# Four of the eight up tiles of each first quarter computed as two seven-product pairs, in a two-layer streaming encoder on one Trainium2 core

## The chip, the core and the metric

The kernel runs on one core of one Trainium2 chip. The metric is the time of one execution on the device, in microseconds (us). The engines are called TensorE (PE in the profile, with PEld for its weight loads), VectorE (DVE), ScalarE (ACT), GpSimd (POOL) and SyncE (SP, which only issues transfers here).

## The reference, cut to what matters

The reference is one step of a two-layer encoder on 576 tokens (512 of a prompt, 64 of a running stream). Each layer has a mixer and then an MLP, and the change is in the MLP alone:

```python
def _rmsnorm(x, g):
    xf = xf * lax.rsqrt(jnp.mean(xf * xf, axis=-1, keepdims=True) + EPS)
    return (xf * g.astype(jnp.float32)).astype(x.dtype)

def _mlp(h, w_up, w_down):
    u = jax.nn.relu(h @ w_up)
    return (u * u) @ w_down
...
    x = x + _mlp(_rmsnorm(x, norm_mlp[i]), mlp_w_up[i], mlp_w_down[i]).astype(x.dtype)
```

The model width is 1024, the hidden width 4096, all in float32.

## The kernel before, in words

**Layout and precision.** x stands as eight blocks of 128 channels x 576 tokens; `HT` = 288 is half of the tokens, so that a half fits one matmul. Every operand of a product is held as two parts, an upper one (a rounded copy, made by ScalarE) and a lower one (what the rounding lost, made by a subtraction on VectorE). A product then takes three matmuls of 128x288: upper x upper, upper x lower, lower x upper. In the names, `wh` and `wl` are the parts of a weight tile of 128x512, `raw` is what a transfer loaded, `xs` are the eight blocks of x times the norm's gain, with both parts.

**The norm.** The MLP runs on x times the gain; the factor per token is multiplied in later. `Norm.add` squares the blocks of x on ScalarE and adds them up in `s2` on VectorE (L344). `Norm.stats` sums `s2` over the channels by ten small matmuls (`st`, L376), from which the factor r is made in small steps on VectorE (L398 to L403); `Norm.spread` spreads it over the partitions by a diagonal (L366, L369) and matmuls with ones (`rb`, L356), which ScalarE copies to `norm.rb` (rbm). TensorE's instructions run in their order, so the up tiles behind `st` wait for the last addition to `s2`.

**Quarters, tiles and pairs.** The hidden width is worked in four quarters of 1024, each with eight up tiles of 128 hidden channels and then four Down pairs of two output tiles. A plain up tile (`project`, L326) goes over all eight blocks of x: 8 x 3 x 2 halves = 48 matmuls. Two tiles can also be computed together as a pair of seven products instead of eight (`seven`, L528): the two tiles and the two halves of tokens make a 2 x 2 product, and sums of weight blocks and sums of x stand in the factors named b11, t1, t2, b21, t3, b22, t4. Each product is 4 blocks x 3 = 12 matmuls; the pair has 84 where two plain tiles have 96. In the first four sevens of each MLP (`SEEDED`) one matmul more seeds a bank. The products use the banks a, b and c of PSUM, the on-chip accumulator memory: the product t4 goes to the bank b that t3 had, after VectorE has read it (L669 in `Up.hi1`).

Quarters 2 to 4 use pairs both for the up tiles (class `Up`) and for Down (class `Down`). The first quarter of each MLP uses eight plain up tiles, then four Down pairs. The relu and squaring of a plain tile are in `finished`, which also makes the sums of the activations that Down needs.

**The sums of x.** A pair of up tiles needs, for each j from 0 to 3, sums of the blocks x[j] and x[4+j]. `x_sums` makes them: one ScalarE instruction, four on VectorE of 128x288 (L451 to L454), a ScalarE cast of the upper part and the lower part on VectorE (L456, 128x864). `x_difference` splits one more of them into `xs` (L313). Before the change j = 0 and 1 are made after the fourth and sixth plain tile, j = 2 and 3 between the Down pairs (`x_prepared`).

**Weights.** The list `jobs` (`mlp_jobs`) fixes the order of the loads; "up" and "down" are plain tiles, "even" and "odd" the two blocks of a pair. `Stream.fill` issues loads as buffers come free: SyncE's queue has the plain ones, and a pair also needs three sums of blocks, for which GpSimd's queue issues accumulating transfers (L235, L256). `made` yields the split units; a subtraction can be given to GpSimd by `sub=pool`. The line is L194 on either engine. In layer 0 the first three up tiles are split early, their lower parts on GpSimd.

Within the MLP the scheduler of the language sets the order on each engine, from the order of the code and the dependences; the engines then run their rows in that order.

Of the kernel before, what the change touches and what calls it, by code (L numbers as in the profile page):

```python
# [18 lines left out]
KT = D // P  # L19
# [33 lines left out]
SEEDED = 4  # L53
LEAD = 5
UP_ORDER = (0, 4, 1, 5, 2, 6, 3, 7)
FACTORS = ("t4", "t3", "t1", "t2", "b11", "b22", "b21")
FIRST_DOWN = (0, 2, 1, 3)

# [2 lines left out]
def pool_dsa_kernel(ctx: ExitStack, tc: tile.TileContext, a, o):  # L61
# [100 lines left out]
    def mlp_jobs(layer, plain=0):  # L162
        for c in range(4):
            for n, f in enumerate(UP_ORDER):
                kind = "odd" if c and n % 2 else "even" if c else "up"
                jobs.append((kind, a["w_up"][layer, c * 8 + f], KT * P))
            for m in range(KT) if c else [2 * q + i for q in FIRST_DOWN for i in range(2)]:
                kind = "down" if c == 3 and m >= KT - plain else "odd" if m % 2 else "even"
                jobs.append((kind, a["w_down"][layer, c, m], KT * P))
# [27 lines left out]
    class Stream:  # L197
# [13 lines left out]
        def fill(self):  # L211
            while jobs:
                kind, src, n = jobs[0]
                mlp = kind in MLP_BLOCKS
                room = self.room(mlp)
                if room is None:
                    return
                at, pool_, size = room
                if not self.blocks or len(self.blocks[-1][1]) == 2:
                    self.blocks.append((kind, [], src, []))  # L220
                raw = self.blocks[-1][1]
                i = len(raw)
                raw.append(raw_tile(pool_, size)[:, :n // 2])
                self.live[at].append(raw[-1])
                if kind == "w_v":
                    act.dma_start(raw[-1].rearrange("p (k c) -> p k c", k=2), src.rearrange("p (k c) -> p k c", k=4)[:, 2 * i:2 * i + 2, :256])
                else:
                    (nc.sync if mlp else act).dma_start(raw[-1], src[:, i * n // 2:(i + 1) * n // 2])
                if kind == "w_ki":
                    weigh = a["w_v"][i].rearrange("p (k c) -> p k c", k=4)[:, :, 256:]  # L230
                    act.dma_start(raw[-1].rearrange("p (k c) -> p k c", k=4)[:, :, 64:64 + NIDX], weigh)
                if kind == "even" and i == 0:
                    self.even, self.sum = src, sum_of(jobs[1][1])
                if kind == "odd" and i == 0:
                    pool.dma_start(raw[0], self.even[:, :512], accum_op=ALU.add)  # L235
                    self.blocks[-1][3].append(self.sum)
                if i:
                    jobs.pop(0)
# [20 lines left out]
    def made():  # L259

        stream = Stream()
        while True:
            block = stream.take()
            if block is None:
                return
            kind, raw = block[:2]
            if kind != "even":
                early = kind == "w_o" and turns["out"] < KT  # L270
                turns["out"] += kind == "w_o"
                for i in range(2):
                    u = split_unit(raw[i], kind == "w_kq" and i == 0 and turns["spare"] < SPARE_UNITS, pool if early or kind == "w_kq" and i else None,
                                   pool.tensor_copy if early and i else act.copy)
                    stream.done(raw[i])
                    yield u
                continue
            _, other, _, (s1,) = stream.take()
            (a11, a12), (s3, a22) = raw, other
            s2 = phase["sums"].tile([P, 512], F32, tag="sum", name=uid("sum"))  # L280
            dve.tensor_tensor(s2, s1, a11, ALU.add)
            for n, src in enumerate((a11, s1, s2, a12, s3, s2, a22)):
                u = split_unit(src)
                if n == 3:
                    dve.tensor_tensor(s2, s2, a12, ALU.add)
                if n in (0, 3, 4, 6):
                    stream.done(src)
                yield u
# [129 lines left out]
    def mlp(layer, gi, late=0, end=None):  # L418
# [23 lines left out]

            return (KT - LAST if end and c == 3 else KT) // 2

        def x_sums(j, raw, first, difference):

            t = x_sums_tile()
            xt.append(t)
            gain, minus = gv[:, gi, j:j + 1], negative[:, half + j:half + j + 1]
            act.activation(first, x[j][:, :HT], AF.Copy, scale=gain)  # L450
            dve.scalar_tensor_tensor(raw[:, 0], x[j][:, HT:], gain, first, ALU.mult, ALU.subtract)  # L451
            dve.scalar_tensor_tensor(difference, x[half + j][:, :HT], gv[:, gi, half + j:half + j + 1], first, ALU.mult, ALU.subtract)
            dve.scalar_tensor_tensor(raw[:, 1], x[half + j][:, :HT], minus, raw[:, 0], ALU.mult, ALU.subtract)
            dve.scalar_tensor_tensor(raw[:, 2], x[half + j][:, HT:], minus, raw[:, 1], ALU.mult, ALU.subtract)  # L454
            act.copy(t[:, :, 0], raw)
            dve.tensor_tensor(t[:, :, 1], raw, f32(t[:, :, 0]), ALU.subtract)  # L456

        def x_difference(j, difference):

# [251 lines left out]
        def finished(i, pt, us):  # L711
# [2 lines left out]
                pair = tiles()  # L714
            v, u = pair
            activated(pt, v[:, 5:7] if i % 2 else v[:, 1:5:3])
            if i == KT - 2:
                parts_of(u, v, slice(4, 5))
                first_sum(v)
                parts_of(u, v, slice(2, 3))  # L720
            elif i == KT - 1:
                middle_sums(v)
                parts_of(u, v, slice(1, 4, 2))
                upper(u, v, slice(5, 7))
                last_sum(v)
                lower(u, v, slice(5, 7))
                parts_of(u, v, slice(0, 1))
            elif i % 2:
                upper(u, v, slice(4, 7))
                first_sum(v)  # L730
                middle_sums(v)
# [5 lines left out]
                us.append(u)  # L737

        todo, us = [], []
        for i in range(KT):  # L740
            w = next_block()
            pt = (psum1("up"), psum1("up")) if i == 2 else psum("up")
            project(pt, w, xs, spread() if i == 2 else iter(()))
            todo.append((i, pt, us))
            if i == 1:
                norm.stats()
            if i < 2:
                continue
            for t in todo:
                finished(*t)  # L750
            todo.clear()
            if i in (3, 5):
                r = 2 * i - 6
                if i == 3:
                    snap = halves(tmp("snap", "s2", 1))
                x_sums(i // 2 - 1, rough[:, r:r + 3], rough[:, r + 3], snap[:, i // 2 - 1])

        def x_prepared(n):

            if n < 2:  # L760
                v = v_tile()
                x_difference(n, snap[:, n])
                x_sums(n + 2, v[:, :3], v[:, 3], v[:, 4])
                x_difference(n + 2, v[:, 4])

        for n, q in enumerate(FIRST_DOWN):
            seven(of(us), n == 0, Down(q))
            x_prepared(n)
        for c in range(1, 4):
            us = []  # L770
            for j in range(half):
# [930 lines left out]
```

## Time and profile before

| | us |
|---|---|
| median of 3 runs | 1071.96 (1071.82 to 1073.69) |
| profiled execution, its own time | 1070.67 |
| its span in the trace | 1068.8 |
| TensorE busy | 1046.4 |
| VectorE busy | 912.0 |
| ScalarE busy | 625.7 |
| GpSimd busy | 239.5 |

The profile is of one execution. A row of a timeline has the start in us from the span's start, the length in us, engine, line of the kernel, operation, output<-inputs, tile, xcount where equal ones are put together, and in brackets the idle time ahead of it with what ended it. A row's length reaches a little over the start of the next, so starts are compared where an instruction's cost is meant. A row of the groups has line, engine, operation, count, then the busy time and the mean of one in ns. Granted clock is the share of full speed at which TensorE was clocked.

### The profile page before, as it was taken

To read this page: it belongs to the slowest core of one execution; us is meant where nothing else is said; L and a number is where in the kernel's file an instruction comes from. 1 tells how busy PE (TensorE), PEld (TensorE's weight loads), DVE (VectorE), ACT (ScalarE), POOL (GpSimd) and SP (SyncE) were. 2 spreads that over 40 slices of the span, in tenths; PEclk is the share of its full clock that TensorE was granted. 3 is DMA by queue.
4 is the path that set the end of the run, shared out by engine and by line. 5 is a ranking of instruction groups with operands and counts; after the bars stand their busy time and mean duration, and the time that the engine had idled before them with its cause. 6 is when DMAs were issued, how large, how long until landed. Compare 5 with 4: busy or idle time off the path is not lost.

```text
span 1068.8 us, 21707 instructions
## 1 busy us (share of the span) xinstructions
PE 1046.4 (98%) x7978; PEld 1022.7 (96%) x7978; DVE 912.0 (85%) x1865; ACT 625.7 (59%) x1252; POOL 239.5 (22%) x254
## 2 busy tenths in 40 slices
PE   8999999999999999999999999999999999999996
PEld 8999999999999999999999888999999999999995
DVE  7879989879988998889999675689889879979974
ACT  8556457547646765454368776456457447547742
POOL 3200111111111110667546620000111111111101
PEclk9999999999999999999999999999999999999998
DMA  8233666676576665845552554343666676676522
GB/s 254 89 102 92 165 165 163 158 179 156 151 182 169 157 173 176 237 137 139 170 156 75 169 170 107 126 107 89 178 159 149 178 172 164 149 183 163 124 55 89
DMA packets 98027, 159.65 MB, mean 149 GB/s; under 512 B 15697, under 2 KB 29312, under 8 KB 97920
## 3 DMA queue, kind: packets, MB, share of 16 engines
q1 hardware_dynamic: 70720, 111.78, 33.2%
q0 software_dynamic: 15840, 28.84, 17.1%
q10 hardware_dynamic: 11360, 17.63, 5.1%
q8 instruction: 63, 1.03, 0.4%
q14 instruction: 44, 0.36, 0.1%
HBM read 142.99 MB, written 12.72 MB: 146 GB/s over the span
## 4 chain that ended last, share of the span: by engine, by line
PE 84%; DVE 7%; DMA 3%; issue 2%; POOL 2%; ACT 1%; SPq 0%; ACTq 0%; DVEq 0%; POOLq 0%
PE b L528 33%; PE c L528 16%; PE up L326 9%; PE a L528 8%; PE pj L326 4%; PE wo L326 2%; PE wa L326 2%; PE pb L1072 1%; PE pt L1402 1%; PE dn L326 1%; PE o L1434 1%; DVE mask L1319 1%; PE sc L1376 1%; DVE m L1318 1%; DMA raw<-in_w_in 1%
## 5 line engine op out<-in xcount | busy, mean ns | idle before, releaser
L193 ACT CAST wh<-raw 128x512 fp32r<-128x512 f32 x308 | 189.7, 620 | 208.5 <-PE b L528 65.9
L194 DVE TENSOR_TENSOR wl<-raw,wh 128x512 fp32r<-128x512 f32 x284 | 198.2, 700 | 33.6 <-ACT wh L193 29.5
L528 PE MATMUL b<-u,wh 128*128 128x288 f32 x992 | 203.3, 296 | 2.3 <-ACT a L565 1.9
L528 PEld LDWEIGHTS b<-u,wh 128*128 128x128 f32 x992 | 159.6, 188 | 4.3 <-ACT a L565 3.1
L193 ACT CAST wh<-sum 128x512 fp32r<-128x512 f32 x165 | 102.3, 620 | 95.7 <-PE b L528 41.6
L528 PE MATMUL b<-u,wl 128*128 128x288 f32 x496 | 145.9, 295 | 0.4 <-DVE wl L194 0.4
L194 DVE TENSOR_TENSOR wl<-sum,wh 128x512 fp32r<-128x512 f32 x165 | 112.2, 686 | 22.3 <-ACT wh L193 20.8
L256 POOL DMA_DIRECT2D sum<-in_w_down x31 | 27.1, 894 | 340.9 <-DMA sum<-in_w_down 102.5
L528 PE MATMUL c<-u,wh 128*128 128x288 f32 x496 | 102.7, 296 | 0.0
L528 PEld LDWEIGHTS b<-u,wl 128*128 128x128 f32 x496 | 93.5, 189 | 0.6 <-DVE wl L194 0.6
L326 PE MATMUL up<-xs,wh 128*128 128x288 f32 x512 | 89.6, 296 | 0.9 <-DVE x L1593 0.8
L494 DVE TENSOR_TENSOR u<-v,u 128x576 fp32r<-128x576 f32 (+3 forms) x106 | 83.0, 786 | 2.0 <-ACT u L491 1.6
L528 PEld LDWEIGHTS c<-u,wh 128*128 128x128 f32 x496 | 79.8, 188 | 1.3 <-ACT wh L193 1.1
L528 PE MATMUL b<-xt,wh 128*128 128x288 f32 x384 | 77.7, 296 | 0.0
L528 PE MATMUL b<-xs,wh 128*128 128x288 f32 x384 | 77.2, 295 | 0.0
L326 PEld LDWEIGHTS up<-xs,wh 128*128 128x128 f32 x512 | 74.6, 188 | 2.0 <-ACT wh L193 1.0
L491 ACT CAST u<-v 128x576 fp32r<-128x576 f32 (+3 forms) x106 | 73.7, 699 | 3.2 <-DVE v L515 2.3
L528 PE MATMUL c<-u,wl 128*128 128x288 f32 x248 | 73.1, 295 | 0.0
L256 POOL DMA_DIRECT2D sum<-in_w_up x24 | 20.8, 865 | 203.1 <-DVE wl L194 83.4
L326 PE MATMUL pj<-xs,wh 128*128 128x288 f32 x352 | 62.1, 295 | 0.0
L528 PEld LDWEIGHTS b<-xt,wh 128*128 128x128 f32 x384 | 61.5, 188 | 0.0
L528 PEld LDWEIGHTS b<-xs,wh 128*128 128x128 f32 x384 | 61.2, 188 | 0.0
(300 smaller groups left out, 2724.7 us busy)
## 6 DMA issues: line engine op xcount, KB each, us to landing
raw<-in_w_up SPq DMA_DIRECT2D x128, 256.0 KB, 3.1
raw<-in_w_down SPq DMA_DIRECT2D x128, 256.0 KB, 2.9
raw<-in_w_o ACTq DMA_DIRECT2D x32, 256.0 KB, 2.8
sum<-in_w_down SPq DMA_DIRECT2D x31, 256.0 KB, 2.9
sum<-in_w_down POOLq DMA_DIRECT2D x31, 256.0 KB, 4.7
raw<-in_w_down POOLq DMA_DIRECT2D x31, 256.0 KB, 5.0
raw<-in_w_in ACTq DMA_DIRECT2D x30, 256.0 KB, 3.0
sum<-in_w_up SPq DMA_DIRECT2D x24, 256.0 KB, 3.2
```

What stands on the lines that cost most here:

```text
L193: cast(h, src)
L194: (sub or how["sub"]).tensor_tensor(l, src, f32(h), ALU.subtract)
L256: pool.dma_start(s1, odd[:, 512:], accum_op=ALU.add)
L326: pe.matmul(pt[h][:, :m] if isinstance(pt, tuple) else pt[:, h, :m], wt, xs[k][:, part, c:c + m], start=(k == 0 and i == 0), stop=(k == n ...
L491: return act.copy(u[:, f, 0], v[:, f])
L494: return dve.tensor_tensor(u[:, f, 1], v[:, f], f32(u[:, f, 0]), ALU.subtract)
L528: ins = pe.matmul(bank[:, :HT], wt, ut, start=first and j == 0 and i == 0, stop=j == 3 and i == 2, skip_group_check=True)
L1072: pe.matmul(pt[:, c0:c0 + rhs.shape[1]], lhs, rhs, start=n == 0, stop=n == len(steps) - 1)
L1318: dve.max(m8[rows], order[rows])
L1319: dve.match_replace(order[rows], m8[rows], order[rows], TAKEN)
L1376: pe.matmul(pt[:, hh, :nw], q[:, 2 * s + hh], ks[g][:, part, :nw], start=part == 0, stop=part == 1)
L1402: pe.transpose(pp[:, c:c + P], pr[:, hh, kt * P:(kt + 1) * P], ident)
```

## The change

In each first quarter only the first four up tiles stay plain (`PLAIN_UP`); the tiles five to eight become two pairs, `Up(0, 2)` and `Up(0, 3)`. The sums of x are therefore needed earlier: `x_sums(j)` is called after each plain tile j, the differences follow the fourth, and `x_prepared` is gone. The lower part of the sums is made on GpSimd instead of VectorE (L466), and of the second, third and fourth plain tile the second half block's lower part is too (`POOLED`). In layer 0 GpSimd made both lower parts of the first three tiles before the change already. All sums go through one tile `rough`, whose slots j = 2 takes over from j = 0, and 3 from 1. The loads of the last four tiles are of the kinds "even" and "odd", and `fill` does not start a pair's loads until the pool for the sums of blocks is open.

```diff
+PLAIN_UP = 4
+POOLED = (1, 2, 3)
...
-                kind = "odd" if c and n % 2 else "even" if c else "up"
+                kind = "up" if not c and n < PLAIN_UP else "odd" if n % 2 else "even"
...
+                if kind == "even" and "sums" not in phase:
+                    return
...
+                if kind == "up":
+                    ups += 1
+                pooled = kind == "up" and (ups - 1) % PLAIN_UP in POOLED
                 for i in range(2):
-                    u = split_unit(raw[i], kind == "w_kq" and i == 0 and turns["spare"] < SPARE_UNITS, pool if early or kind == "w_kq" and i else None,
+                    u = split_unit(raw[i], kind == "w_kq" and i == 0 and turns["spare"] < SPARE_UNITS, pool if early or i and (pooled or kind == "w_kq") else None,
...
-        def x_sums(j, raw, first, difference):
+        def x_sums(j):
...
+            at = half * (1 + j % 2)
+            raw, first, difference = rough[:, at:at + 3], rough[:, at + 3], rough[:, j]
...
             act.copy(t[:, :, 0], raw)
-            dve.tensor_tensor(t[:, :, 1], raw, f32(t[:, :, 0]), ALU.subtract)
+            pool.tensor_tensor(t[:, :, 1], raw, f32(t[:, :, 0]), ALU.subtract)
...
-        for i in range(KT):
+        for i in range(PLAIN_UP):
...
-            if i < 2:
-                continue
-            for t in todo:
-                finished(*t)
-            todo.clear()
-            if i in (3, 5):
-                r = 2 * i - 6
-                if i == 3:
-                    snap = halves(tmp("snap", "s2", 1))
-                x_sums(i // 2 - 1, rough[:, r:r + 3], rough[:, r + 3], snap[:, i // 2 - 1])
...
-        for n, q in enumerate(FIRST_DOWN):
-            seven(of(us), n == 0, Down(q))
-            x_prepared(n)
+            if i >= 2:
+                for t in todo:
+                    finished(*t)
+                todo.clear()
+            x_sums(i)
+        snap = halves(tmp("snap", "s2", 1))
+        for j in range(half):
+            x_difference(j, rough[:, j])
+        for j in range(PLAIN_UP // 2, half):
+            up = Up(0, j)
+            seven(of_x, False, up)
+            us.append(up.u)
+
+        for q in FIRST_DOWN:
+            seven(of(us), q == FIRST_DOWN[0], Down(q))
```

The lines of the new kernel are shifted: the split of a weight is L196, the addition of squares L352, `x_sums` L461 to L466, the products L538, the read of bank b ahead of t4 L679.

The order shows what moves. First VectorE in layer 0, around the last additions to `s2` (s_113), as it was; `xt_...` is the scratch that holds a block's squares, `wl_...` a weight's lower part:

```order
L344 TENSOR_TENSOR s_113_641<-s_113_641,xt_674 128x576
L194 TENSOR_TENSOR wl_737<-raw_371,wh_736 128x512
L344 TENSOR_TENSOR s_113_641<-s_113_641,xt_674 128x576 x2
L344 TENSOR_TENSOR s_113_641<-s_113_641,xt_681 128x576
L194 TENSOR_TENSOR wl_743<-raw_377,wh_742 128x512
```

The same place with the change (`s_108` is the new name of `s2`, `rough` the tile of the sums of x):

```order
L352 TENSOR_TENSOR s_108_631<-s_108_631,xt_664 128x576
L463 SCALAR_TENSOR_TENSOR rough_676<-x_83,negative_674,rough_676 128x288
L324 SCALAR_TENSOR_TENSOR xs_653<-x_84,gv,xs_653 128x576
L464 SCALAR_TENSOR_TENSOR rough_676<-x_83,negative_674,rough_676 128x288
L196 TENSOR_TENSOR wl_752<-raw_371,wh_751 128x512
L462 SCALAR_TENSOR_TENSOR rough_676<-x_84,gv,rough_676 128x288 x2
L352 TENSOR_TENSOR s_108_631<-s_108_631,xt_664 128x576
L464 SCALAR_TENSOR_TENSOR rough_676<-x_83,negative_674,rough_676 128x288
L352 TENSOR_TENSOR s_108_631<-s_108_631,xt_664 128x576
L196 TENSOR_TENSOR wl_844<-raw_734,wh_843 128x512
L352 TENSOR_TENSOR s_108_631<-s_108_631,xt_671 128x576
```

Ten sums of x (five of them ahead of this piece) and one more lower part of a weight now stand ahead of the last addition.

GpSimd after the change, from the end of the weights that it split early, in layer 0:

```order
L260 DMA sum_950<-in_w_down 128x512
L239 DMA raw_741<-in_w_up 128x512
L196 TENSOR_TENSOR wl_758<-raw_377,wh_757 128x512
L466 TENSOR_TENSOR xt_726<-rough_676,xt_726 128x3x288
L239 DMA raw_761<-in_w_up 128x512
L466 TENSOR_TENSOR xt_833<-rough_676,xt_833 128x3x288
L466 TENSOR_TENSOR xt_931<-rough_676,xt_931 128x3x288
L466 TENSOR_TENSOR xt_1012<-rough_676,xt_1012 128x3x288
L260 DMA sum_1180<-in_w_down 128x512
```

Before, only transfers stood here; now one lower part of a weight and the four of the sums do, and the accumulating transfers queue between them.

TensorE after the change, around the last plain tile of layer 0; `rb` are the matmuls that spread r, `b_1031` is the first product of the first pair, which the scheduler put ahead of that tile, `a_1032` the seed:

```order
L334 MATMUL up_854<-xs_653,wl_396 128x288
L364 MATMUL rb_888<-xt_671,ones 128x288
L364 MATMUL rb_891<-xt_671,ones 128x288
L538 MATMUL b_1031<-xs_632,wh_843 128x288 x2
L538 MATMUL b_1031<-xs_632,wl_844 128x288
...
L538 MATMUL b_1031<-xs_641,wl_844 128x288
L574 MATMUL a_1032<-xs_632,wh_843 128x288
L334 MATMUL up_953<-xs_632,wh_751 128x288 x4
```

Before, the matmuls rb stood inside the third tile and the fourth followed it directly; now rb follows the third tile, and thirteen matmuls of the pair come between rb and the fourth.

More of the change, by code (lines that the diff above doesn't have):

```diff
@@ L263, in made @@
         stream = Stream()
+        ups = 0
         while True:
@@ L716, in finished @@
             activated(pt, v[:, 5:7] if i % 2 else v[:, 1:5:3])
[L717 to L728, printed above, removed]
+            if i % 2:
                 upper(u, v, slice(4, 7))
@@ L746, in mlp @@
                 norm.stats()
-            if i < 2:
-                continue
-            for t in todo:
-                finished(*t)
-            todo.clear()
-            if i in (3, 5):
-                r = 2 * i - 6
-                if i == 3:
-                    snap = halves(tmp("snap", "s2", 1))
-                x_sums(i // 2 - 1, rough[:, r:r + 3], rough[:, r + 3], snap[:, i // 2 - 1])
[L758 to L764, printed above, removed]
-        for n, q in enumerate(FIRST_DOWN):
-            seven(of(us), n == 0, Down(q))
-            x_prepared(n)
+            if i >= 2:
[12 more added lines that the diff above has]
+            seven(of(us), q == FIRST_DOWN[0], Down(q))
         for c in range(1, 4):
```

## The prediction

> **What bounds the kernel now.** I read the page first, for which engine sets the end, then the busy time of each engine in the two stretches that the change touches, then the timeline of TensorE and VectorE in them.
>
> ```profile
> span 1068.8 us, 21707 instructions
> ...
> PE 1046.4 (98%) x7978; PEld 1022.7 (96%) x7978; DVE 912.0 (85%) x1865; ACT 625.7 (59%) x1252; POOL 239.5 (22%) x254
> ...
> PE 84%; DVE 7%; DMA 3%; issue 2%; POOL 2%; ACT 1%; SPq 0%; ACTq 0%; DVEq 0%; POOLq 0%
> ```
>
> TensorE is busy for 98% of the span and carries 84% of the chain that ended last. A matmul taken away is worth its time, if whatever feeds TensorE keeps up. The second view has the stretch of the first quarter's up tiles in layer 0 (41.0 to 95.3) and in layer 1 (679 to 737); its columns are length, busy PE, PEld, DVE, ACT and POOL with counts, granted clock, DMA share and GB/s.
>
> ```profile
> 41.00:95.30 54.30, 54.22 (x407) 53.55 (x406) 44.64 (x78) 29.21 (x49) 2.61 (x3) 1.00 0.29 79
> ...
> 679.00:737.00 58.00, 57.22 (x425) 56.36 (x426) 42.36 (x78) 29.18 (x49) 2.59 (x3) 1.00 0.34 92
> ```
>
> TensorE has no gap there, but VectorE is busy for 82% of the first stretch. GpSimd, which takes the new work, does almost nothing. The change therefore asks whether VectorE, made to do its work earlier, stays ahead of TensorE. The timeline shows how far ahead it is in layer 0.
>
> ```profile
> 41.38 0.77 PE L326 MATMUL up<-xs,wh 128*128 128x288 f32 x4
> ...
> 54.15 1.34 PE L376 MATMUL st<-ones,s 128*128 128x96 f32 x10
> 55.41 0.80 PE L326 MATMUL up<-xs,wh 128*128 128x288 f32 x4
> ...
> 60.67 1.13 PE L356 MATMUL rb<-xt,ones 128*128 128x288 f32 x4
> 61.43 0.51 PE L326 MATMUL up<-xs,wh 128*128 128x288 f32 x1
> ...
> 47.56 0.69 DVE L194 TENSOR_TENSOR wl<-raw,wh 128x512 fp32r<-128x512 f32 x1
> 48.16 2.34 DVE L344 TENSOR_TENSOR s<-s,xt 128x576 f32<-128x576 f32 x3
> 50.42 0.68 DVE L194 TENSOR_TENSOR wl<-raw,wh 128x512 fp32r<-128x512 f32 x1
> ```
>
> The statistics matmuls (st) at 54.15 need the last addition of the squares, which is over by 50.42. The slack is 3.7 us. In layer 1 it is much larger, 691.99 less 681.46:
>
> ```profile
> 680.71 0.75 DVE L344 TENSOR_TENSOR s<-s,xt 128x576 f32<-128x576 f32 x1
> ...
> 691.99 1.34 PE L376 MATMUL st<-ones,s 128*128 128x96 f32 x10
> 693.25 0.80 PE L326 MATMUL up<-xs,wh 128*128 128x288 f32 x4
> ```
>
> **The matmuls saved.** Between 41.38 and 54.15 two plain tiles, 96 matmuls, pass: 12.77 us / 96 = 0.133 us each. Two plain tiles become one pair of seven products, 7 x 12 = 84 matmuls, so a pair saves 12 x 0.133 = 1.6 us. There are two pairs in each of the two MLPs: 3.2 us a layer, **-6.4 us** in all. The seed matmul goes with the first four sevens of an MLP wherever they are, and their number stays.
>
> **What VectorE now does ahead of the statistics, layer 0.** By the order, ten of the sums of x (L461 to L464) and one more subtraction of a weight's lower part stand ahead of the last addition of squares. Their durations, start to start:
>
> ```profile
> 73.70 0.52 DVE L451 SCALAR_TENSOR_TENSOR rough<-x,gv,rough 128x288 f32<-128x288 f32 x1
> 74.14 0.51 DVE L452 SCALAR_TENSOR_TENSOR snap<-x,gv,rough 128x288 f32<-128x288 f32 x1
> ...
> 80.88 1.05 DVE L456 TENSOR_TENSOR xt<-rough,xt 128x864 fp32r<-128x864 f32 x1
> 81.85 0.45 DVE L502 TENSOR_TENSOR v<-v 128x288 f32<-128x288 f32 x1
> ```
>
> A sum takes 0.43 us, and the subtraction 48.16 - 47.56 = 0.60. Ten and one make 4.9 us, so the last addition is over at 55.3 in place of 50.42, and TensorE, which is there at 54.15, waits 1.2 us. That is without GpSimd.
>
> **What GpSimd's instructions cost VectorE.** GpSimd now makes the lower parts of the sums (L466, 128x864) and, new in layer 0, one lower part of a weight; in layer 1 three of these. Their durations follow from the groups:
>
> ```profile
> L194 POOL TENSOR_TENSOR wl<-raw,wh 128x512 fp32r<-128x512 f32 x32 | 41.1, 1300 | 20.6 <-ACT wh L193 17.2 <-DMA qi<-qi 3.3
> ...
> L1178 POOL TENSOR_TENSOR rp<-rp,sn 128x576 f32<-128x576 f32 x4 | 5.7, 1437 | 0.0
> ```
>
> The first is 1.3 us (1.25 in the stretch without waits); 288 elements more than 576 at the slope of the two rows give an estimate of 2.1 us for L466. VectorE does the same in 0.60 and 0.97. GpSimd has the time; what matters is what VectorE does meanwhile. One place of the trace has both at work on operands that all lie in SBUF:
>
> ```profile
> 440.42 1.29 POOL L194 TENSOR_TENSOR wl<-raw,wh 128x512 fp32r<-128x512 f32 x1 [3.31 <-DMA qi<-qi]
> 442.52 1.76 POOL L1241 TENSOR_TENSOR cs<-cs,rba 128x576 f32<-128x576 f32 x1 [0.81 <-DMA qi<-qi]
> ...
> 439.85 0.69 DVE L194 TENSOR_TENSOR w<-raw,w 128x512 fp32r<-128x512 f32 x1 [0.84 <-ACT w L193]
> 440.46 1.86 DVE L1180 TENSOR_TENSOR rp<-rp,rp 128x576 f32<-128x576 f32 x1
> 442.25 0.74 DVE L1181 TENSOR_TENSOR rp<-rp,rp 128x576 f32<-128x576 f32 x1
> 442.91 1.98 DVE L1242 TENSOR_TENSOR sn<-sn,rba 128x576 f32<-128x576 f32 x1
> ```
>
> The same 128x576 form takes VectorE 0.74 us alone, and 1.86 and 1.98 while GpSimd's instruction runs: the difference, 1.1 and 1.2 us, is what was left of GpSimd's. GpSimd's 1.76 began inside VectorE's 0.74 and is longer by the rest of it. They take turns, an instruction at a time. The Trainium skill ("SBUF — State Buffer", section "SBUF: two separate sides") says that the port pair the two share is an exclusive lock held for a whole instruction, which a VectorE instruction with two SBUF inputs needs as well; these rows agree, and by it each GpSimd instruction costs VectorE at most its full time. Sums, lower parts and additions of squares all have two inputs in SBUF; the multiplications by rbm, which read PSUM, have one. So I price each GpSimd instruction between nothing (VectorE idle just then) and its whole duration, and take the whole where VectorE has a queue.
>
> **Layer 0, the first wait.** Ahead of the last addition lie the weight's lower part (1.25) and L466 of j=0 (2.1) for certain. L466 of j=1 can start after the sum of row L464 of j=1 and ScalarE's cast, with three VectorE instructions (0.75, 0.60 and 0.75) left up to the end of the last addition: half of it, 1.05 (0 to 2.1). 1.2 + 1.25 + 2.1 + 1.05 = **5.6 us** that TensorE waits at st (1.2 to 6.6). The small steps to the diagonal and six sums follow (5.6 us) while TensorE does st and a whole tile (7.6 us), so rb itself is in time. Then the first pair's b11 needs a bank that ScalarE's copies of rb give back: 0 to 0.9 us, I take **0.45**.
>
> **Layer 0, the second wait.** The product t4 of the first pair needs the bank that VectorE empties at L679. From st to there TensorE has 26.45 us of work: st 1.26, two tiles 12.7, rb 0.75, the bank 0.45, thirteen matmuls 1.73, six products 9.55. VectorE's rows in between are priced by the durations above and these:
>
> ```profile
> 56.91 0.69 DVE L366 TENSOR_TENSOR xt<-ident,r 128x512 f32<-128x512 f32 x1
> 57.52 0.25 DVE L369 TENSOR_SCALAR xt<-ident,r 128x64 f32<-128x64 f32 x1
> ...
> 62.27 1.42 DVE L480 SCALAR_TENSOR_TENSOR v<-up,rbm 128x576 f32<-128x576 f32 x2 [2.26 <-ACT rbm L357]
> ...
> 65.15 0.45 DVE L512 TENSOR_TENSOR v<-v 128x288 f32<-128x288 f32 x1
> 65.51 0.45 DVE L515 SCALAR_TENSOR_TENSOR v<-v 128x288 f32<-128x288 f32 x1
> 65.88 1.05 DVE L494 TENSOR_TENSOR u<-v,u 128x864 fp32r<-128x864 f32 x1
> 67.19 1.36 DVE L494 TENSOR_TENSOR u<-v,u 128x1152 fp32r<-128x1152 f32 x1 [0.25 <-ACT u L491]
> ```
>
> Fifteen of 128x512 (weights' lower parts and sums of blocks) at 0.60 are 9.0; six sums of x 2.6; small steps and diagonal 2.0; the multiplications by rbm 2.75; twelve of 128x288 at 0.37, 4.4; two each of 128x864 (0.97) and 128x1152 (1.27) 4.5; one of 128x576 0.75: 26.0 us. To them comes the wait for rbm, up to 2.26, and of the two L466 left (j=2, 3) one that falls into that wait and one, 2.1, that doesn't. 26.0 + 2.26 + 2.1 - 26.45 = 3.9 at most, nothing at least; I take **2.5**. Layer 0: -3.2 + 5.6 + 0.45 + 2.5 = **+5.35 us**.
>
> **Layer 1.** At st there are 10.5 us of slack, so all sums fit ahead of it. At rb, VectorE has, counted in the same way, 13.4 us of instructions from 679.0 and, ahead of the diagonal, GpSimd's two to three weight parts and three L466 (2 x 1.25 + 3 x 2.1 = 8.8): 701.2. TensorE reaches rb after st and a whole tile, 693.25 + 6.35 = 699.6 with the few tenths that it wins by starting undelayed, 699.2: **2.1** of wait (0 to 3.4). The bank **0.45** again. Then 20.2 us of VectorE and one L466 of 2.1 against 18.8 of TensorE to t4: **3.5** (1.4 to 5.7). Layer 1: -3.2 + 2.1 + 0.45 + 3.5 = **+2.85**.
>
> **The clock.** A wait of some us has a second price, read at the end of the span, where the last matmul is over by 1058.95:
>
> ```profile
> 1057.71 1.24 PE L815 MATMUL rb<-room,ones 96*128 96x288 f32 x4
> ...
> 1060.00:1064.00 4.00, 0.00 (x0) 0.00 (x0) 1.14 (x3) 0.00 (x0) 1.01 (x2) 0.75 0.92 291
> 1064.00:1068.80 4.80, 0.00 (x0) 0.00 (x0) 0.00 (x0) 0.00 (x0) 0.00 (x0) 0.50 0.01 3
> ```
>
> A mean of 0.75 over 1060 to 1064 is full clock until 1062 and half after it: it falls some 3 us after the last work. A first wait of 5.6 us would cross that. How long the half clock lasts when work returns no row here shows; 0 to 2 us lost, I take **1.0**. The Trainium skill ("TensorE: Matmul & The Clock Gate", Part 1) has the clock come back after some 3.4 us of sustained work; by it the loss would be an estimated 1.7, and the sum 0.7 higher.
>
> **Edits at nothing.** A pair loads seven half blocks where two tiles loaded four; with a DMA share of 0.29 these hide behind the other traffic. GpSimd's accumulating loads now stand behind L466 in its queue and start some 2 us later, ahead of a use some 30 us on. SP's loads keep their order beside them. ScalarE makes the same casts, earlier, at 29 us of 54. What used to lie in the first Down (sums, differences) leaves VectorE there, but TensorE's wait in it is small and not VectorE's:
>
> ```profile
> 98.88 0.54 PE L528 MATMUL b<-u,wh 128*128 128x288 f32 x2 [0.48 <-ACT a L565]
> ```
>
> That, 0.5 us in each layer, may go or stay.
>
> **Sum.** 5.35 + 2.85 + 1.0 = +9.2 us on the profiled execution, whose own time is 1070.67 (span 1068.8 and 1.87 around it): 1079.9. It lies 1.3 below the median of the three runs, 1071.96, so against that **1081**. About 0.2%, 2.1 us, is what a measurement of this kernel can tell from no change.
>
> **The rivals.**
> - *The two engines hardly meet.* If GpSimd's instructions fall into idle time of VectorE, layer 0 is -3.2 + 1.2 + 0.45 + 1.5 = 0 and layer 1 -3.2 + 0.45 + 1.5 = -1.25: 1070.7, no change. For it: VectorE has 18% idle. Against: that idle lies mostly after 50.4, and the sums now fill it. Chance 0.15.
> - *Faster: TensorE never waits.* VectorE's 0.75 us additions of squares run ahead by more than I think, and the bank at t4 comes in time because the multiplications by rbm are done early. Then only the two 0.45 are paid: 1071.96 - 6.4 + 0.9 = 1066.5. It decides for this when the last addition is over by 54.15 and L679 starts within TensorE's 26.45 us. For it: GpSimd takes 4 x 0.97 us from VectorE in each layer. Against: the order of VectorE's rows. Chance 0.13.
> - *Only the first wait.* L466 of j=0 and the weight part meet the additions, but the second waits are hidden: -6.4 + 0.9 + 5.6 + 2.1 + 1.0 + some 1 = +4.2, 1076. Chance 0.12.
> - *The forecast*, with the clock falling or not, 1079 to 1085. Chance 0.60.
>
> **How the numbers follow.** 1070 takes in the case without change; 1088 is the forecast with the ends of its bounds that can hold together (j=1 whole +1.05, clock +1, both t4 waits at their ends +3.6, +1.3 at rb). Left out are the faster case and a few hundredths above. Faster 0.13, within 0.2% 0.15, slower 0.72.
>
> **What would show it.** In the profile after: TensorE with a wait of several us on VectorE's addition of squares ahead of st in layer 0; VectorE's rows L352, L462 or L196 of over 1.5 us beside GpSimd's L466 of about 2.1; a wait for the bank ahead of the first pair's t4 in each layer; a granted clock below 1.00 just behind the first wait; 48 matmuls fewer. The prediction is wrong if VectorE's instructions keep their 0.4 to 0.75 us beside L466, or if st in layer 0 starts by 55.

## The result, and the profile after

| | us |
|---|---|
| before, median of 4 runs | 1071.89 (1071.31 to 1073.69) |
| after, median of 4 runs | 1078.82 (1076.54 to 1080.64) |
| after against before | 1.0067 (95% interval 1.0055 to 1.0079) |
| after, profiled execution | 1079.79 (span 1078.0) |

The change makes the kernel 0.67% slower, 6.9 us; 1081 was forecast. The page of the changed kernel, to be held against the one before:

```profile
span 1078.0 us, 21735 instructions
...
PE 1048.1 (97%) x7930; PEld 1023.4 (95%) x7930; DVE 934.9 (87%) x1891; ACT 636.6 (59%) x1288; POOL 268.4 (25%) x274
```

There are 48 matmuls fewer (7978 to 7930), and yet TensorE is busy 1.7 us longer: the matmuls that are left took more time. VectorE is busy for 22.9 us more, although it has only 26 more instructions. The table of TensorE's waits (what it waited for: us in total, times, longest) has three new rows on top, and one row of before that has almost gone:

```profile
PE st L384 <- DVE s L352: 5.3, 1, 5.3
PE a L574 <- DVE v L660: 5.0, 2, 2.8
...
PE rb L364 <- DVE xt L374: 1.5, 1, 1.5
...
PE b L538 <- ACT a L575: 0.3, 1, 0.3
```

In the same table of the kernel before, the last one is:

```profile
PE b L528 <- ACT a L565: 1.9, 4, 0.5
```

**The first wait** is where the prediction had it, in layer 0 ahead of st. TensorE's timeline after:

```profile
54.10 0.43 PE L334 MATMUL up<-xs,wl 128*128 128x288 f32 x2
59.84 2.53 PE L384 MATMUL st<-ones,s 128*128 128x96 f32 x10 [5.32 <-DVE s L352]
62.30 1.33 PE L334 MATMUL up<-xs,wh 128*128 128x288 f32 x4
```

GpSimd's and VectorE's rows ahead of that show why the last addition of squares came so late:

```profile
50.54 1.86 POOL L196 TENSOR_TENSOR wl<-raw,wh 128x512 fp32r<-128x512 f32 x1 [12.69 <-ACT wh L195]
52.36 2.25 POOL L466 TENSOR_TENSOR xt<-rough,xt 128x864 fp32r<-128x864 f32 x1
...
57.07 2.10 POOL L466 TENSOR_TENSOR xt<-rough,xt 128x864 fp32r<-128x864 f32 x1 [0.69 <-ACT xt L465]
```

```profile
50.56 0.69 DVE L196 TENSOR_TENSOR wl<-raw,wh 128x512 fp32r<-128x512 f32 x1
51.17 3.77 DVE L462 SCALAR_TENSOR_TENSOR rough<-x,gv,rough 128x288 f32<-128x288 f32 x2
54.86 0.75 DVE L352 TENSOR_TENSOR s<-s,xt 128x576 f32<-128x576 f32 x1
...
56.62 0.68 DVE L196 TENSOR_TENSOR wl<-raw,wh 128x512 fp32r<-128x512 f32 x1
57.23 2.56 DVE L352 TENSOR_TENSOR s<-s,xt 128x576 f32<-128x576 f32 x1
```

This is how such a turn is read. Two sums of 0.43 us took 3.77 together, up to 54.86: the stretch covers GpSimd's weight part (to 52.40) and its first L466 (to 54.6). The last addition, 0.75 alone, took 2.56 because the second L466 began at 57.07, just ahead of it. VectorE shows no idle time here; it counts as busy while it is held up. So a group's mean that has grown, with a GpSimd row beside it, is the sign, not a wait.

**The clock** is the dearest single term in the trace, and the prediction had it at 1.0 us. Windows around the first wait (the last three columns are granted clock, DMA share, GB/s):

```profile
57.00:58.00 1.00, 0.00 (x0) 0.00 (x0) 1.00 (x2) 0.50 (x1) 0.93 (x1) 1.00 0.98 147
58.00:59.00 1.00, 0.00 (x0) 0.00 (x0) 1.00 (x1) 0.00 (x0) 1.00 (x1) 0.91 0.98 166
59.00:60.00 1.00, 0.16 (x1) 0.16 (x1) 1.00 (x2) 0.00 (x0) 0.17 (x1) 0.50 0.61 211
...
64.00:65.00 1.00, 1.00 (x6) 1.00 (x6) 1.00 (x2) 0.00 (x0) 1.00 (x1) 0.50 0.00 0
65.00:66.00 1.00, 1.00 (x7) 1.00 (x6) 1.00 (x2) 0.00 (x0) 1.00 (x1) 0.68 0.00 0
66.00:67.00 1.00, 1.00 (x10) 1.00 (x9) 1.00 (x5) 0.00 (x0) 0.01 (x1) 1.00 0.00 0
```

From 58.8 to 65.6 TensorE runs at half clock, and for 5.8 us of that it has work. The st matmuls take 2.5 us instead of 1.3, the next sixteen matmuls 3.7 instead of 2.1: 2.8 us lost. The same happens behind the second waits, at the seed matmul of the second pair, which stands right ahead of the first pair's t4, in layer 0 (91.47) and in layer 1 (731.86):

```profile
91.47 0.40 PE L574 MATMUL a<-xs,wh 128*128 128x288 f32 x1 [2.20 <-DVE v L660]
```

```profile
93.00:94.00 1.00, 1.00 (x7) 1.00 (x6) 0.99 (x2) 1.00 (x4) 0.00 (x0) 0.50 0.18 51
...
95.00:96.00 1.00, 1.00 (x6) 1.00 (x6) 1.00 (x4) 0.44 (x1) 0.00 (x0) 0.50 0.38 129
96.00:97.00 1.00, 1.00 (x8) 1.00 (x8) 0.99 (x2) 1.00 (x3) 0.00 (x0) 0.82 0.02 8
```

A wait of 2.2 us was enough here to halve the clock for 3.4 us, at a loss of 1.5 us; behind the 2.84 us in layer 1 it was halved for 6.8, at a loss of 2.6. Both losses are taken from the starts: the seed and the 24 matmuls behind it pass in 5.2 and 6.3 us, and in 3.7 in each layer of the run warm_gate below, where the clock stays at 1.00. The windows of layer 1:

```profile
731.00:734.00 3.00, 2.14 (x8) 2.06 (x9) 2.81 (x7) 1.93 (x5) 0.00 (x0) 0.54 0.45 157
734.00:737.00 3.00, 3.00 (x15) 3.00 (x14) 2.08 (x6) 1.73 (x4) 0.00 (x0) 0.50 0.27 87
737.00:740.00 3.00, 3.00 (x21) 3.00 (x21) 2.99 (x7) 2.52 (x5) 0.86 (x1) 0.82 0.45 62
```
The Trainium skill ("TensorE: Matmul & The Clock Gate", Part 1) has the clock fall after an idle window of some 3.4 us; here a shorter wait did it, and the measurement decides. That the low stretches last about 3.4 us or twice that agrees with that page's window. What decides whether a shorter wait does it is taken up in the last section.

**The end.** The last matmuls rb start 12.0 us later than before, yet the span is only 9.2 us longer:

```profile
1069.70 1.24 PE L807 MATMUL rb<-room,ones 96*128 96x288 f32 x4
```

From there to the end of the span it is 8.3 us; before it was 1068.8 - 1057.71 = 11.1. The last large transfers stop 6.4 us behind that row in both traces, so the 2.8 us lie in the idle stretch after them. This came back in the experiments, and is taken up there.

### The profile page after: what moved, and what is told of

Its sections match the earlier page's. It is cut to its first block, busy times and chain, and to the rows that moved or that the text cites. A ratio compares the mean times of both kernels' runs of the same rounds, so it can differ in the third digit from the quotient of the medians.

```text
span 1078.0 us, 21735 instructions
## 1 busy us (share of the span) xinstructions
PE 1048.1 (97%) x7930; PEld 1023.4 (95%) x7930; DVE 934.9 (87%) x1891; ACT 636.6 (59%) x1288; POOL 268.4 (25%) x274
## 5 line engine op out<-in xcount | busy, mean ns | idle before, releaser
L196 DVE TENSOR_TENSOR wl<-raw,wh 128x512 fp32r<-128x512 f32 x280 | 197.2, 706 | 18.7 <-ACT wh L195 14.2
L538 PE MATMUL b<-u,wh 128*128 128x288 f32 x992 | 203.2, 296 | 0.8 <-DVE u L504 0.4
L538 PEld LDWEIGHTS b<-u,wh 128*128 128x128 f32 x992 | 159.8, 188 | 2.1 <-ACT a L575 0.8
L538 PE MATMUL b<-u,wl 128*128 128x288 f32 x496 | 145.9, 295 | 0.4 <-DVE wl L196 0.4
L196 DVE TENSOR_TENSOR wl<-sum,wh 128x512 fp32r<-128x512 f32 x177 | 121.9, 694 | 25.1 <-ACT wh L195 23.6
L538 PE MATMUL c<-u,wh 128*128 128x288 f32 x496 | 102.9, 296 | 0.2 <-DVE x L622 0.2
L538 PEld LDWEIGHTS b<-u,wl 128*128 128x128 f32 x496 | 93.5, 189 | 0.6 <-DVE wl L196 0.6
L538 PE MATMUL b<-xt,wh 128*128 128x288 f32 x448 | 92.4, 300 | 0.0
L538 PE MATMUL b<-xs,wh 128*128 128x288 f32 x448 | 90.1, 295 | 0.0
L504 DVE TENSOR_TENSOR u<-v,u 128x576 fp32r<-128x576 f32 (+2 forms) x108 | 83.4, 774 | 4.8 <-ACT u L501 4.3
L538 PEld LDWEIGHTS c<-u,wh 128*128 128x128 f32 x496 | 79.7, 188 | 1.7 <-ACT wh L195 1.5
L501 ACT CAST u<-v 128x576 fp32r<-128x576 f32 (+2 forms) x108 | 74.3, 690 | 6.4 <-DVE v L525 3.4
L538 PEld LDWEIGHTS b<-xt,wh 128*128 128x128 f32 x448 | 73.1, 192 | 0.3 <-DVE v L679 0.2
L538 PE MATMUL c<-u,wl 128*128 128x288 f32 x248 | 73.2, 295 | 0.0
L538 PEld LDWEIGHTS b<-xs,wh 128*128 128x128 f32 x448 | 71.3, 188 | 0.5 <-ACT rbm L365 0.5
L538 PE MATMUL b<-xt,wl 128*128 128x288 f32 x224 | 67.0, 299 | 0.0
L538 PE MATMUL b<-xs,wl 128*128 128x288 f32 x224 | 64.0, 295 | 0.0
L482 ACT ACTIVATE v<-v 128x288 f32<-128x288 f32 (+1 forms) x120 | 53.5, 458 | 14.6 <-DVE v L660 13.4
```

The lines of the kernel that those rows point to most:

```text
L196: (sub or how["sub"]).tensor_tensor(l, src, f32(h), ALU.subtract)
L482: act.activation(v, v, AF.Square)
L501: return act.copy(u[:, f, 0], v[:, f])
L504: return dve.tensor_tensor(u[:, f, 1], v[:, f], f32(u[:, f, 0]), ALU.subtract)
L538: ins = pe.matmul(bank[:, :HT], wt, ut, start=first and j == 0 and i == 0, stop=j == 3 and i == 2, skip_group_check=True)
```

## The experiments

Theory A is the prediction's: GpSimd and VectorE take turns, and each GpSimd instruction costs VectorE its own duration. Theory B leaves GpSimd free of blame. C and D ask whether VectorE's order or its whole load is the bound, E what the clock costs by itself. Each run is compared with runs of the kernel before on the same chip; medians in us.

**L466 on VectorE again.**

```diff
-            pool.tensor_tensor(t[:, :, 1], raw, f32(t[:, :, 0]), ALU.subtract)
+            dve.tensor_tensor(t[:, :, 1], raw, f32(t[:, :, 0]), ALU.subtract)
```

> The changed kernel with one edit: the lower parts of the sums of x (L466) are made on VectorE again. Theory A (turns at the shared access: each L466 on GpSimd holds VectorE up for its 2.1 us): on VectorE it costs 0.97, so about 1.1 us is won for each one on the path. The wait at st falls little, 5.3 to about 4.8, since two L466 now stand ahead of the last addition on VectorE itself; the wait at rb in layer 1 (1.5) goes; the waits ahead of t4 (2.2 and 2.8) fall to about 1 and with them the half clock behind them. 1073, between 1070 and 1076. Theory B (GpSimd's part is free, only VectorE's order costs): VectorE gets eight times 0.97 more work in front of TensorE, so slower than the changed kernel, 1080 or more.

Measured: 1077.28 against 1071.82, ratio 1.0050 (1.0035 to 1.0065). That is neither: it is under the 1080 of B, but above the 1070 to 1076 of A, and its interval overlaps that of the change (1.0055 to 1.0079).

```profile
58.80 2.53 PE L384 MATMUL st<-ones,s 128*128 128x96 f32 x10 [4.11 <-DVE s L352]
68.94 1.13 PE L364 MATMUL rb<-xt,ones 128*128 128x288 f32 x4
...
91.88 0.40 PE L574 MATMUL a<-xs,wh 128*128 128x288 f32 x1 [3.51 <-DVE v L660]
```

```profile
70.54 1.42 DVE L490 SCALAR_TENSOR_TENSOR v<-up,rbm 128x576 f32<-128x576 f32 x2 [2.06 <-ACT rbm L365]
```

The wait at st falls by 1.2 us, the one at rb in layer 1 goes, and of the long VectorE rows ahead of the seed only the one beside the weight part is left. But 4.1 us are still enough to halve the clock, TensorE reaches rb only at 68.94, and now it is VectorE that waits for rbm, 2.06 us, and the seed comes no earlier than in the changed kernel (91.88 against 91.47). What VectorE won in time it lost again waiting for TensorE. The second waits are thus 3.51 and 2.12 us, where about 1 was expected, and the clock falls behind both.

**All new work on VectorE** (the edit above, and `POOLED = ()`).

> The changed kernel with nothing of the MLPs' new work on GpSimd: L466 and the weights' lower parts of the plain tiles all on VectorE. Theory A: no VectorE row over 1.5 us is left in the stretch; the wait at st is made of VectorE's own rows, 1.2 + 0.6 (weight) + 1.9 (two L466) + about 1 that the order puts there = 4.8; waits ahead of t4 of about 1. Some 1073, within 2 us of the run with only L466 moved. Theory B: slower than that run by the four weights' parts, 0.6 each, and slower than the changed kernel.

Measured: 1074.25, ratio 1.0021 (1.0011 to 1.0031). Faster than with the weights' parts on GpSimd, where B wanted it slower: 4.6 us of the change's 6.9 went with GpSimd's new work, partly through the clock, which falls behind fewer waits here (at st and in layer 1). A had the run within 2 us of the one before it; it is 3.0 faster, so the four weights' parts cost more than A had put them at. In the table of waits, 4.3 us are left at st, and 3.8 at the two seeds:

```profile
PE st L384 <- DVE s L352: 4.3, 1, 4.3
PE a L574 <- DVE v L660: 3.8, 2, 2.1
```

The wait at st is thus almost as long without GpSimd: by now two L466 stand in VectorE's own queue ahead of the last addition.

**Sums behind the last addition of squares.** `Norm.add` keeps its last addition as `self.at`, and

```diff
-            x_sums(i)
+            if i < half:
+                with behind([norm.at.ins]):
+                    x_sums(i)
```

> The changed kernel, with the sums of x put behind the last addition of squares on VectorE by an order edge; GpSimd's work stays. Theory C (the order is what costs in layer 0): the wait at st of 5.3 us and the half clock behind it (2.7) go, and the time falls by about 8 us to 1071. Theory D (VectorE as a whole is the bound from the first tile to the first pair's t4: it was idle for only some 3 us of the 50 before that product): the wait moves from st to rb and t4; VectorE's row L679 in layer 0 still comes at about 88 to 91 us, TensorE waits there for 6 us or more, and the time falls by 3 us at most, 1076 to 1079.

Measured: 1074.43, ratio 1.0024 (1.0013 to 1.0035): between C and D, with D's mechanism. st starts at 54.92, but the wait turns up further on, in four pieces:

```profile
63.63 1.24 PE L364 MATMUL rb<-xt,ones 128*128 128x288 f32 x4 [0.83 <-DVE xt L374]
67.07 0.54 PE L538 MATMUL b<-xs,wh 128*128 128x288 f32 x2 [2.20 <-ACT rbm L365]
70.27 0.79 PE L334 MATMUL up<-xs,wh 128*128 128x288 f32 x4 [1.21 <-DVE v L490]
88.80 0.40 PE L574 MATMUL a<-xs,wh 128*128 128x288 f32 x1 [2.35 <-DVE v L660]
```

They are 6.6 us, against 7.5 with the sums early. What is gained is the clock, more than the wait: of its three falls one is left, behind the seed's 2.35 us, and the waits of 2.20 us here and of 2.22 at the seed in layer 1 leave it at 1.00.

**Both: order edge, and all on VectorE.**

> Both: sums behind the last addition of squares, and all lower parts on VectorE. By A and D together, VectorE loses the 8.0 us that its long rows beside GpSimd cost in layer 0 up to t4 and gets 4.5 us of work for it, so L679 comes 3.5 us earlier than in the changed kernel, at about 85 to 88; TensorE waits there some 4 us in layer 0 and about 1 in layer 1: 1071, between 1068 and 1074. By C alone (no bound by VectorE) 1071.9 - 6.4 = 1065.5. By B it is slower than the run with the order edge alone.

Measured: 1069.18, ratio 0.9969 (0.9958 to 0.9981), faster than the kernel before. The seed's bank comes at 85.6, as A and D worked out, and layer 0 keeps one long wait, at rb, with 3.4 us of half clock behind it:

```profile
64.62 1.24 PE L364 MATMUL rb<-xt,ones 128*128 128x288 f32 x4 [2.46 <-DVE xt L374]
85.61 0.40 PE L574 MATMUL a<-xs,wh 128*128 128x288 f32 x1 [0.34 <-DVE v L660]
```

What GpSimd's part costs by itself, its clock included, is the difference to the run before this one: 1074.4 to 1069.2, 5.2 us.

**Early sums without the pairs** (`PLAIN_UP = 8`, and `x_sums(i)` for i < 4 alone).

> The changed kernel with all eight up tiles plain: the early sums of x and GpSimd's parts stay, the pairs (and their saving of 6.4 us, and the waits ahead of the first pair's t4) are gone. Theory A and C: the wait at st in layer 0 stays, 4 to 6 us, with the half clock of 2.8 us behind it, and nothing pays for it; no wait at t4, since VectorE has the whole quarter to catch up: 1078 to 1082. If the early sums cost nothing by themselves, and only the pairs bring the waits, 1072.

Measured: 1083.68, ratio 1.0103 (1.0087 to 1.0118), a little above the range. The first wait is there (3.8 us, st at 57.93) with a granted clock of 0.73 and 0.77 in the windows 54 to 59 and 59 to 68, there is none at a seed, and nothing pays for it. The run does not price the early sums alone, though: `finished` had an order of its own for the last two plain tiles, which the changed kernel has no more and this run does not bring back. TensorE now waits 0.80 and 0.74 us in the first Down of layer 0, and the clock falls there a second time (107.5 to 110.9).

**Six plain tiles, one pair**, order edge and all on VectorE (`PLAIN_UP = 6`).

> Six plain tiles and one pair, sums behind the last addition of squares, all lower parts on VectorE. Half the saving (3.2 us), and TensorE has 12.7 us more of its own work ahead of the pair's t4, of which VectorE's new work takes some 7. Theory D (VectorE is the bound only up to t4): no wait at t4 in either layer, rb still late by some 2 us in layer 0: 1069 less or more 1.5, about the same as four plain tiles with the same edits (1069.2). If the waits at t4 were not VectorE's backlog, they stay, and it is 1071 or more.

Measured: 1069.35, ratio 0.9977 (0.9966 to 0.9989), as D had it. No wait at a seed or t4 in either layer; the fourth tile waits 1.28 us for its bank in both (2.6 in all).

**Filling the second waits.** In `seven`, for the second pair, `FILL` = 20, ordered behind the first pair's b22 and ahead of the seed; the columns written are read by nothing:

```diff
+                    for _ in range(FILL):
+                        d = pe.matmul(b[:, HT:], w[0][:, :P], operand(0, "b11", 0)[:, :512 - HT], start=False, stop=False, skip_group_check=True)
```

> The changed kernel with 20 matmuls of 224 columns (2 us of TensorE) that nothing reads, put ahead of the seed of the second pair in each layer, where TensorE waits 2.2 and 2.8 us for VectorE's L660. Theory E (the half clock behind those two waits costs 1.7 and 3.1 us of its own): the granted clock stays 1.00 behind them and the time falls by 3 to 5 us, to 1074 to 1076, though not one wait of VectorE is shorter. If the half clock costs nothing because VectorE is late anyway, the time stays at 1079.

Measured: 1077.05 (1075.34 to 1077.95), ratio 1.0041 (1.0026 to 1.0057). That is above the 1074 to 1076 expected. The medians are 1.8 us apart, and the two kernels' runs overlap; in the traces the last matmuls rb come 3.0 us earlier (1066.71 against 1069.70). The row of the 20 matmuls and the window behind it:

```profile
89.02 2.39 PE L579 MATMUL b<-xs,wh 128*128 128x224 f32 x20
```

```profile
88.00:100.00 12.00, 12.00 (x92) 11.65 (x92) 12.00 (x22) 8.01 (x18) 1.49 (x2) 1.00 0.42 113
```

The clock stays at 1.00, where it fell without them, though from b22 to the seed it is no shorter (2.4 and 3.0 us, against waits of 2.2 and 2.8): the fall costs time of its own. By the starts it is 1.5 and 2.6 us at the two places, of which 3.0 are left at the last matmuls rb; the run times bear the direction out, and less of the size.

**The kernel before, with its lower parts on GpSimd.** The edit of the first experiment the other way round, at L456.

> The kernel before with one edit: the lower parts of its sums of x (L456) on GpSimd instead of VectorE, where they were made, after the fourth and sixth plain tile and in the first Down. Theory A: VectorE's rows beside them show up to 2 us more, but VectorE is nowhere so late there that TensorE waits: no change, 1071 to 1073. If GpSimd's work costs TensorE something directly, 2 us or more for each layer: 1076. The stretch from the last matmuls rb to the end tells, too, whether its 11.1 us in the profile of before, against 8.3 in every changed kernel, belong to the kernel before.

Measured: 1068.55, ratio 0.9971 (0.9959 to 0.9982): a gain where none was expected. The turns are there, for instance a sum of activations of 0.45 us that takes 2.14 beside L456:

```profile
80.59 2.37 POOL L456 TENSOR_TENSOR xt<-rough,xt 128x864 fp32r<-128x864 f32 x1 [12.44 <-ACT xt L455]
```

```profile
81.12 2.14 DVE L502 TENSOR_TENSOR v<-v 128x288 f32<-128x288 f32 x1
```

No wait of TensorE follows from it, and the four waits of 0.5 us ahead of the Down products' t2 are gone from the table; 2.1 us are won by the last matmuls rb (1055.58). Why those four go is not shown. So the same move of work is a gain in this kernel, where VectorE has time, and a loss in the changed one, where TensorE waits for its next row. The end takes 11.0 us here, 11.0 with eight plain tiles too, 8.3 in every kernel with two pairs in the first quarter, 8.5 to 8.6 with one. The 2.5 to 2.8 us belong to kernels with pairs there; what they are is open, since the trace shows nothing but the last transfers and then an idle stretch.

**Sums behind the norm's diagonal** (six plain tiles; the weights' lower parts on VectorE, those of the sums on GpSimd; `turns["diag"]` keeps the last instruction of the diagonal, and the sums for j = 0, 1 are called after the relus of the third tile, for j = 2, 3 after those of the fourth).

> Six plain tiles, one pair; the sums of x put behind the diagonal of the norm on VectorE, so that neither st nor rb can wait for them; their lower parts on GpSimd, the weights' lower parts on VectorE. Theory: what made the change slow is only that sums and GpSimd's work lay ahead of st and rb; behind the diagonal VectorE has the time of three tiles for them. No wait of TensorE over 0.5 us in the stretch in either layer; the matmuls rb come at about 60.7 in layer 0; 3.2 us saved against the kernel before, about 2 from the four waits of 0.5 that the move of the lower parts to GpSimd took out of it: 1066, between 1064 and 1068. If the pair by itself brings waits that its saving doesn't pay, 1068.5 or more, the time of the kernel before with only its lower parts on GpSimd.

Measured: 1092.68, ratio 1.0190 (1.0172 to 1.0207). The theory falls: moved as late as this, the sums aren't there when the pair's product t1 wants them, one j after the other, the clock falls again, and GpSimd's L466 itself lies on that path:

```profile
91.68 0.40 PE L538 MATMUL c<-xt,wh 128*128 128x288 f32 x1 [3.56 <-ACT xt L465]
94.33 0.61 PE L538 MATMUL c<-xt,wh 128*128 128x288 f32 x1 [2.12 <-POOL xt L466]
97.70 0.61 PE L538 MATMUL c<-xt,wh 128*128 128x288 f32 x1 [1.25 <-POOL xt L466]
```

**The same on VectorE.**

> The same with the lower parts on VectorE. Where VectorE has the time, GpSimd's turns (2.1 us for each) against VectorE's own 0.97 matter little, either way: within 1.5 us of the run with them on GpSimd, and no VectorE row over 1.5 us. If GpSimd's turns still cost there, this one is the faster by 2 us or more.

Measured: 1080.94, ratio 1.0086 (1.0066 to 1.0107). The same waits, shorter (2.31 and 1.63 us in layer 0). GpSimd costs 11.7 us here: TensorE waits for L466 itself, which takes some 2.1 us there instead of 0.97, and the half clock lasts 27.3 us with GpSimd and 13.7 without.

**Sums in two halves** (six plain tiles; j = 0, 1 behind the last addition, j = 2, 3 behind the diagonal but called ahead of the relus; all on VectorE).

```diff
+            if i == 2:
+                with behind([turns["diag"].ins]):
+                    x_sums(2)
+                    x_sums(3)
             if i >= 2:
                 for t in todo:
```

> Six plain tiles, one pair; the sums of x for j = 0 and 1 behind the last addition of squares, for j = 2 and 3 behind the norm's diagonal but ahead of the relus; all lower parts on VectorE. What the earlier runs ask for: st waits for nothing, the diagonal has only half of the sums in front of it, and the sums are all there well ahead of the pair's t1. Waits of about 1 us in layer 0 (rb or the bank of the fourth tile), none at t1 and t4; 3.2 us of matmuls and 2.7 us at the end saved against the kernel before, less some 2 of waits: 1068, between 1066 and 1070, not above the run with all four sums behind the addition (1069.3). A wait at t1 would show as 1072 or more.

Measured: 1066.90, ratio 0.9953 (0.9940 to 0.9965), the fastest of all, 5.1 us under the kernel before. Of the stretch's waits in layer 0, one of over 0.5 us is left:

```profile
64.16 0.80 PE L334 MATMUL up<-xs,wh 128*128 128x288 f32 x4 [1.34 <-DVE v L490]
```

**The same with the lower parts on GpSimd.**

> The same with the lower parts of the sums on GpSimd. Theory A: each turn of 2.1 us that falls ahead of the diagonal or of the relus makes TensorE wait at rb or at the fourth tile's bank, about 1 to 2 us in layer 0 more than with VectorE's 0.97: 1069 to 1071, slower than the run on VectorE. If GpSimd's help is a gain wherever VectorE isn't late, as in the kernel before with only its lower parts moved, it is the faster one, 1066 to 1067.

Measured: 1071.85, ratio 0.9997 (0.9988 to 1.0005). That wait is 3.97 us now, 2.6 longer, and the clock is halved for 6.8 us beside it: 5.0 us lost by the one line that the change also has. This is the cleanest price of L466 on GpSimd, since the edit is that line alone.

```profile
67.67 1.33 PE L334 MATMUL up<-xs,wh 128*128 128x288 f32 x4 [3.97 <-DVE v L490]
```

## Why the prediction was right, point by point

- **The matmuls saved**, 48, are right.
- **The first wait** was put at 5.6 us and is 5.32, by the instructions that were named: weight part, two L466, ten sums. Its pieces err both ways: the weight part and the first L466 cost VectorE 2.8 us instead of 3.35, the second L466 1.8 instead of 1.05. That the turns are what stretches VectorE is shown by its rows; that GpSimd's part costs time is shown by 5.2 and 5.0 us in two pairs of runs, the clock included. That L466 on VectorE would be much better at this place is not so: with all of it on VectorE, 4.3 us of the wait stay.
- **The bank behind rb**, 0.45 in each layer: in layer 0, rb to the first product takes 1.14 us (70.25 to 71.39) in place of 0.75, so 0.4. In layer 1 three matmuls of the tile stand between rb and the product, and only 0.1 us is lost.
- **The second waits** were put at 2.5 and 3.5 and are 2.20 and 2.84. They are not at the bank of L679, though, but one row ahead of t4, at the seed, whose bank VectorE empties at L660, in the row right above L679 (90.97 and 91.34). In layer 0 the size is in part luck: TensorE took 29.4 us from st to there instead of 26.45, most of it by the half clock, and VectorE took 31.6 us from the last addition to L679, where the forecast comes to 26.45 + 2.5 = 28.9.
- **rb in layer 1**: 2.1 forecast, 1.46 measured.
- **The clock** is the term that was mis-sized: 1.0 was taken for one fall; there are three, with 2.8, 1.5 and 2.6 us lost, 6.9 in all. The step that failed is "crosses that": the 3 us at the end of the trace were taken for a limit (by the raster in the last section they only tell where the next slot began), and only the first wait was held against it. Waits of 2.2 us can bring the fall already.
- **Not foreseen**, the other way: the waits ahead of t2 in the kernel before go (1.9 us, 0.3 left); they were put at 0.5 us in each layer, though the table has four, and "may go or stay" was all that was said. And the end is 2.8 us shorter.

The sum with the measured terms is -6.4 + 5.3 + 1.5 + 5.0 + 0.5 (two banks) + 6.9 - 1.6 - 2.8 = +8.4, where the spans differ by 9.2; 0.8 us is not assigned. The direction is right, and the waits nearly so. That the number came so near is in part luck: the clock was 5.9 us too low, the waits together 2.3 too high, and gains of 4.4 were not foreseen. Even so 1078.8 lies just under the 1079 to 1085 that the forecast gave for its own case.

## What to carry to other kernels

Before work is given to an idle GpSimd, look for what VectorE does at that moment: the same line cost 5 us where TensorE waited for VectorE's next row, and came with a gain of 2 to 3.5 us where it did not. Work that is needed earlier must be put in the queue where its deadline lies between two others, here behind the last addition of squares and ahead of the pair's t1; too early it holds up the norm, too late the product. And a wait of TensorE is priced with the clock that it loses: 7.5 us of waits in layer 0 cost 4 us more in slow matmuls.

## What the runs showed of the hardware

A wait of about 2 us may halve the clock or not, and it isn't the length alone that decides: 1.91 us were followed by a fall in the run plain6_split_dve (642.2), 2.22 in layer 1 of the run behind were not. In the run with all new work on VectorE, a wait of 2.12 us in layer 1 left a mean granted clock of 0.93 in the window 720 to 745; in the run with the order edge too, a wait of the same 2.12 us left 1.00:

```profile
720.00:745.00 25.00, 22.53 (x155) 21.88 (x154) 22.41 (x43) 16.96 (x35) 2.00 (x3) 0.93 0.46 110
```

```profile
720.00:745.00 25.00, 22.03 (x163) 21.48 (x162) 23.11 (x45) 16.97 (x35) 2.47 (x3) 1.00 0.41 110
```

The traces show most of what decides. In the changed kernel the clock changes at 58.82, 65.65, 92.95, 96.36, 731.25 and 738.08 us; the later ones lie 2, 10, 11, 197 and 199 times 3.413 us behind the first. In all eleven traces with a fall ahead of the end the changes lie whole multiples of 3.413 us apart; where the raster starts differs from trace to trace. So a wait counts by how much of one such slot it fills. The 2.12 us with all on VectorE lie in a single slot, 724.0 to 727.4, in which TensorE is busy for 38%, and the clock is halved from 727.4; with the order edge they are split over two slots with 71% and 66%, and it stays. Between 30 and 1050 us of these traces, a slot at full clock with TensorE busy for less than 44% was always followed by half clock, one with 59% or more never; in between both occur.

An instruction of five columns is held up like any other: L410, 128x5, takes 2.00 us beside L466, where it takes 0.17 alone.

```profile
64.03 2.00 DVE L410 TENSOR_TENSOR nt<-nt,ms 128x5 f32<-128x5 f32 x1
```
